# Mixture of experts in a two-block transformer: experts ordered by their tokens, every other one in 64 slots and whole fp32

## Chip, cores and metric

The kernel runs on one core of one Trainium2 chip. The time is that of the device, in microseconds, the median of three runs. One further execution was profiled, and everything about engines and transfers is read from that one.

## The reference

Two transformer blocks follow each other on 256 tokens of width 1024 (and 256 context tokens in the first). The change touches only one step, the mixture of experts in the second layer of the first block:

```python
def swiglu(t, w1, w3, w2):
    return (jax.nn.silu(t @ w1) * (t @ w3)) @ w2

def moe_swiglu(h, w_router, b_router, w1, w3, w2):
    t = h.reshape(-1, shp[-1])
    logits = (t @ w_router).astype(jnp.float32) + b_router.astype(jnp.float32)
    top_v, top_i = lax.top_k(logits, TOP_K)
    top_w = jax.nn.softmax(top_v, axis=-1)
    combine = jnp.sum(jax.nn.one_hot(top_i, N_EXPERTS, dtype=jnp.float32) * top_w[..., None], axis=1)
    y = None
    for e in range(N_EXPERTS):
        ye = combine[:, e:e + 1] * swiglu(t, w1[e], w3[e], w2[e]).astype(jnp.float32)
        y = ye if y is None else y + ye
```

There are 8 experts, each token picks 2, and an expert is 1024 x 2816 twice (w1, w3) and 2816 x 1024 (w2), all in fp32: 34.6 MB.

## The kernel before

Everything is one program whose order on each engine is set by a scheduler that goes by the program's text and its own estimates; each engine then runs its list strictly in that order. Weights come in pieces of 128 x 2048 fp32 (1 MB), issued by SyncE into a ring of raw slots: three slots, and in the expert stage four more (R2), seven in all. Slots are taken in turn, so the load of piece k waits until piece k-7 has left its slot. An expert is 33 pieces: 22 of w1/w3 (each four slices of 128 rows by 256 columns of w1 and 256 of w3) and 11 of w2 (each two slices of 128 rows by 1024 columns).

Products are made to fp32 accuracy out of three faster ones. `piece` (L268) splits a raw piece, 1024 columns at a time, into a high part (ScalarE, L282) and a low part (VectorE, L283), in a second ring `hl` of ten slots, which is room for two and a half pieces; `mm3t` (L294) multiplies high by high, high by low, low by high (L295 to L297), each 128 tokens by 512 columns. I call these split products. A matmul on raw fp32 operands without splitting, a whole product, stands elsewhere in the kernel: in `mod_piece` (L348, four column groups of 32) and in a state sum (L804, two halves of 64 columns).

The stage runs so. The router's scores choose two experts for each token; `sel8` marks them, `rank` numbers the tokens of each expert, `cmb` has their weights. `choice` (L1099) makes `cmb` and `cmax`, the largest count. `gather(e)` (L1120), called for e = 0 and, inside the w2 pass of experts 1, 3 and 5, for the next two, builds a 0/1 matrix `O` of 2 x 128 slots and multiplies it with the split tokens `htk` (L1132, 256 columns), and ScalarE copies the result to `hg` (L1135). Then each expert e, 0 to 7 in that order: 11 steps of two w1/w3 pieces (24 split products into one bank, then silu on ScalarE, the product on VectorE, two transposes on TensorE L1197, and their split L300/L301); then 11 steps of one w2 piece (12 split products, bank S). In step 2 of the next expert, `scatter` (L1138) returns the rows to their tokens, 16 products of 256 columns, and adds them to `accY`. All places have 128 slots. In expert 1 a branch on `cmax` (L1213) calls `overflow`, which would run every expert once more for slots over 128; it is not taken on these inputs. After expert 7 the scatter ends in the residual, the squares of the next norm, and the second block.

## Time and profile before

| | |
|---|---|
| median of 3 runs | 2461.57 us (2458.0 to 2462.22) |
| profiled execution | 2460.61 us |
| its span, first to last instruction | 2458.8 us |
| mean granted TensorE clock | 0.978 of full |
| TensorE busy | 2361.2 us (96%) |
| VectorE, ScalarE busy | 1645.0 us (67%), 1368.0 us (56%) |
| read from HBM | 500.58 MB, 204 GB/s over the span |
| loads of expert weights | 264 of 1024 KB |

Between the span and the execution's time lie 1.8 us. TensorE's busy time is that of overlapping records (a product of 512 columns is drawn with 0.40 us, and the next starts 0.23 us later), so its share says that it always has work, not how much; the distance from start to start is the price of one. The span divides into the first block's two layers up to about 930 us, the experts from 931 to 1751 us, and the second block behind that.

### The profile page before, as it was taken

To read this page: it belongs to the slowest core of one execution; us is meant where nothing else is said; L and a number is where in the kernel's file an instruction comes from. 1 tells how busy PE (TensorE), PEld (TensorE's weight loads), DVE (VectorE), ACT (ScalarE), POOL (GpSimd) and SP (SyncE) were. 2 spreads that over 40 slices of the span, in tenths; PEclk is the share of its full clock that TensorE was granted. 3 is DMA by queue.
4 is the path that set the end of the run, shared out by engine and by line. 5 is a ranking of instruction groups with operands and counts; after the bars stand their busy time and mean duration, and the time that the engine had idled before them with its cause. 6 is when DMAs were issued, how large, how long until landed. Compare 5 with 4: busy or idle time off the path is not lost.

```text
span 2458.8 us, 35481 instructions
## 1 busy us (share of the span) xinstructions
PE 2361.2 (96%) x13906; PEld 2005.0 (82%) x13906; DVE 1645.0 (67%) x2627; ACT 1368.0 (56%) x2186; POOL 5.0 (0%) x12
## 2 busy tenths in 40 slices
PE   6999999999999989999999999999899999999997
PEld 4887777888778877877777788777799999898997
DVE  5655553333366558987988898889766776667765
ACT  4445542232354567876767777677645554455543
POOL 0000000000000000000000000000000000000000
PEclk9999899999999989999999999999999999999999
DMA  8232233333333367987998998888543454333552
GB/s 286 93 122 72 101 120 137 114 127 107 133 113 121 130 235 281 369 318 294 337 352 330 339 346 341 337 348 333 197 146 138 155 188 171 124 144 138 189 180 95
DMA packets 72839, 503.98 MB, mean 205 GB/s; under 512 B 8102, under 2 KB 10188, under 8 KB 14940
## 3 DMA queue, kind: packets, MB, share of 16 engines
q1 hardware_dynamic: 72012, 499.82, 54.9%
q8 instruction: 111, 1.82, 0.3%
q0 software_dynamic: 368, 1.43, 0.2%
q10 hardware_dynamic: 288, 0.41, 0.1%
q14 instruction: 60, 0.49, 0.1%
HBM read 500.58 MB, written 1.06 MB: 204 GB/s over the span
## 4 chain that ended last, share of the span: by engine, by line
PE 49%; DVE 3%; ACT 2%; issue 1%; ACTq 0%; DVEq 0%
PE bkA L290 6%; PE bkA L291 6%; PE bkA L292 6%; PE bkA L296 5%; PE bkA L297 4%; PE bkA L295 4%; PE bkS L295 3%; PE bkS L296 3%; PE bkS L297 3%; PE bkS L290 2%; PE bkS L292 2%; PE bkS L291 2%; DVE hl L283 2%; ACT hl L282 1%; PE bkT L1197 1%
## 5 line engine op out<-in xcount | busy, mean ns | idle before, releaser
L283 DVE TENSOR_TENSOR hl<-raw,hl 128x1024 fp32r<-128x1024 f32 (+2 forms) x861 | 1012.6, 1202 | 386.5 <-ACT hl L282 377.3
L282 ACT CAST hl<-raw 128x1024 fp32r<-128x1024 f32 (+2 forms) x861 | 867.8, 1039 | 424.2 <-PE bkS L291 153.1
L290 PE MATMUL bkA<-ph,hl 128*128 128x256 f32 x1080 | 309.9, 288 | 5.2 <-ACT ph L1356 4.5
L291 PE MATMUL bkA<-pl,hl 128*128 128x256 f32 x1080 | 307.6, 285 | 0.0
L292 PE MATMUL bkA<-ph,hl 128*128 128x256 f32 x1080 | 306.5, 284 | 0.0
L296 PE MATMUL bkA<-hl,hg 128*128 128x512 f32 x704 | 284.3, 404 | 7.1 <-DVE hl L283 5.3
L295 PE MATMUL bkA<-hl,hg 128*128 128x512 f32 x704 | 281.5, 400 | 0.9 <-ACT hl L282 0.9
L297 PE MATMUL bkA<-hl,hg 128*128 128x512 f32 x704 | 282.2, 401 | 0.0
L290 PEld LDWEIGHTS bkA<-ph,hl 128*128 128x128 f32 x1080 | 207.7, 193 | 7.8 <-ACT ph L1356 4.9
L291 PEld LDWEIGHTS bkA<-pl,hl 128*128 128x128 f32 x1080 | 208.0, 193 | 0.3
L292 PEld LDWEIGHTS bkA<-ph,hl 128*128 128x128 f32 x1080 | 207.8, 192 | 0.5 <-issue 0.3
L296 PEld LDWEIGHTS bkA<-hl,hg 128*128 128x128 f32 x704 | 132.7, 189 | 50.4 <-DVE hl L283 22.1
L295 PEld LDWEIGHTS bkA<-hl,hg 128*128 128x128 f32 x704 | 132.8, 189 | 30.3 <-ACT hl L282 2.2
L297 PEld LDWEIGHTS bkA<-hl,hg 128*128 128x128 f32 x704 | 132.9, 189 | 27.1
L296 PE MATMUL bkS<-hl,gh 128*128 128x512 f32 x352 | 140.2, 398 | 6.0 <-PEq L1213 5.3
L290 PE MATMUL bkA<-acth,hl 128*128 128x512 f32 (+1 forms) x376 | 138.7, 369 | 4.4 <-ACT acth L459 4.4
L297 PE MATMUL bkS<-hl,gl 128*128 128x512 f32 x352 | 139.2, 395 | 0.0
L292 PE MATMUL bkA<-acth,hl 128*128 128x512 f32 (+1 forms) x376 | 137.6, 366 | 0.0
L291 PE MATMUL bkA<-actl,hl 128*128 128x512 f32 (+1 forms) x376 | 137.0, 365 | 0.0
L290 PE MATMUL bkS<-acth,hl 128*128 128x512 f32 (+1 forms) x312 | 119.6, 384 | 2.8 <-ACT hl L282 2.8
L295 PE MATMUL bkS<-hl,gh 128*128 128x512 f32 x352 | 121.2, 395 | 0.1
L292 PE MATMUL bkS<-acth,hl 128*128 128x512 f32 (+1 forms) x312 | 119.0, 382 | 0.5 <-DVE hl L283 0.5
(496 smaller groups left out, 4154.9 us busy)
## 6 DMA issues: line engine op xcount, KB each, us to landing
raw<-in_exp_w_dram SPq DMA_DIRECT2D x264, 1024.0 KB, 5.7
raw<-in_w_mod_dram SPq DMA_DIRECT2D x48, 1024.0 KB, 4.9
raw<-in_w_up_dram SPq DMA_DIRECT2D x44, 1024.0 KB, 4.8
raw<-in_w_in_dram SPq DMA_DIRECT2D x32, 1024.0 KB, 4.8
raw<-in_ffn_w_dram SPq DMA_DIRECT2D x30, 1024.0 KB, 4.9
raw<-in_w_out_dram SPq DMA_DIRECT2D x16, 1024.0 KB, 4.8
raw<-in_w_down_dram SPq DMA_DIRECT2D x16, 1024.0 KB, 4.8
raw<-in_w_down_dram SPq DMA_DIRECT2D x8, 768.0 KB, 4.3
```

The source lines that it names most:

```text
L282: SC.copy(hi[:, :m], r)
L283: V.tensor_sub(lo[:, :m], r, hi[:, :m].bitcast(F32))
L290: PE.matmul(o, wh, xh, start=start, stop=False)
L291: PE.matmul(o, wh, xl, start=False, stop=False)
L292: PE.matmul(o, wl, xh, start=False, stop=stop)
L295: PE.matmul(o, th, wh, start=start, stop=False)
L296: PE.matmul(o, th, wl, start=False, stop=False)
L297: PE.matmul(o, tl, wh, start=False, stop=stop)
L1197: PE.transpose(pt[:, c * 128:(c + 1) * 128], g[:, c * 128:(c + 1) * 128], ident)
```

## The change

The experts are put in order of their token counts on the chip, after the router. Place 0 stays expert 0; places 1 to 7 go by falling count. `choice` computes each expert's place by comparing counts (some 27 more small VectorE operations), permutes `rank`, `sel8` and `cmb` into `order`, and writes the expert numbers to `idx`. Loop turn e now works on place `PLACES[e]`: even turns on places 0 to 3, odd ones on places 4 to 7. SyncE reads seven numbers from `idx` into registers, and every load for turns 1 to 7 has its address from a register.

Even turns work as before, with 128 slots. Odd turns (`few`) have 64 slots, and nothing is split: the gather adds the high and low parts on VectorE into one fp32 tile `hg1` of 64 slots (L1180), and the raw piece is the moving operand of whole products (L1250, L1302) with 64 columns of weights. Two such products, for the two halves of the columns, go to partitions 0 to 63 and 64 to 127 of one bank. One transpose a step instead of two, one bank for w2 instead of two, no low part of `yh`, and a scatter of 8 whole products with 64 rows each (L1194). The gathers are made in the w2 pass of the even turns, for turns (0), (1, 2), (3, 4), (5, 6), (7), with 128, 192, 192, 192 and 64 columns. The branch moves from turn 1 to turn 2, and compares counts with each place's capacity.

```diff
+PLACES = (0, 4, 1, 5, 2, 6, 3, 7)
...
+        if name.startswith("exp") and layer in expert_at:
+
+            nc.sync.dma_start(raw[:, :n * w], src.rearrange("(e r) -> e r", r=tot)[
+                ds(expert_at[layer], 1), o:o + 128 * n * w].rearrange("e (p k) -> (e p) k", p=128))
+            return raw, n, w
...
+    def whole(name, i, layer):
+        return (ahead.pop((name, i, layer), None) or load(name, i, layer))[0]
...
+            V.scalar_tensor_tensor(key, p[:, 0:8], 8.0, i8, op0=ALU.mult, op1=ALU.subtract)
+            V.memset(key[:, 0:1], 1.0e6)
+            V.tensor_tensor(t8, key[:, None, :].to_broadcast([128, 8, 8]), key[:, :, None].to_broadcast([128, 8, 8]),
+                            op=ALU.is_gt)
+            V.tensor_reduce(place, t8, axis=AX, op=ALU.add)
...
+            for q, x in enumerate((rank, sel8, cmb)):
+                for t in range(2):
+                    V.tensor_mul(t8, pm, x[:, t, None, :].to_broadcast([128, 8, 8]))
+                    V.tensor_reduce(order[:, q, t, :], t8, axis=AX, op=ALU.add)
...
+            V.tensor_copy(idx, key[0:1, :])
...
-        def gather(e):
+        def gather(es):
...
+            lo_, hi_ = (64 if es[0] % 2 else 128), (128 if es[-1] % 2 else 256)
...
-                        PE.matmul(p[:, v * 256:(v + 1) * 256], htk[:, v, t, d * 128:(d + 1) * 128],
-                                  O[:, t].rearrange("p j s -> p (j s)"), start=t == 0, stop=t == 1)
-                for v in range(2):
-                    last[0] = SC.copy(hg[v][:, d].rearrange("p j s -> p (j s)"), p[:, v * 256:(v + 1) * 256])
...
+                        PE.matmul(p[:, v * 256 + lo_:v * 256 + hi_], htk[:, v, t, d * 128:(d + 1) * 128],
+                                  O[:, t].rearrange("p j s -> p (j s)")[:, lo_:hi_], start=t == 0, stop=t == 1)
+                if hg1 is not None:
+                    V.tensor_reduce(hg1[:, d * 64:(d + 1) * 64], p.rearrange("p (v s) -> p s v", v=2)[:, 64:128, :],
+                                    axis=AX, op=ALU.add)
+                for v in range(2 if hg0 is not None else 0):
+                    last[0] = SC.copy(hg0[:, v, d, :], p[:, v * 256 + 128:(v + 1) * 256])
...
+                    if yl is None:
+                        b = slice(64 * (dd // 4), 64 * (dd // 4) + 64)
+                        PE.matmul(o, yh[b, (dd % 4) * 128:(dd % 4 + 1) * 128], OT[b, :].bitcast(F32), start=True, stop=True)
+                        continue
...
+                if few:
+
+                    for k in range(2):
+                        raw = whole("exp_w13", 2 * i + k, e)
+                        for kc in range(4):
+                            w4 = raw[:, kc * 512:(kc + 1) * 512].rearrange("p (m h c) -> p h m c", m=2, h=2)
+                            for h in range(2):
+                                PE.matmul(p[64 * h:64 * h + 64, :256].rearrange("p (m c) -> p m c", m=2),
+                                          hg1[:, (4 * k + kc) * 64:(4 * k + kc + 1) * 64], w4[:, h],
+                                          start=k == 0 and kc == 0, stop=k == 1 and kc == 3)
...
+                if i == 0 and e == 0:
+                    for v in range(1, 8):
+                        expert_at[v] = nc.values_load(idx[0:1, PLACES[v]:PLACES[v] + 1], engines=[mybir.EngineType.SP],
+                                                      min_val=0, max_val=7)
-                if i == IGA and e == 1:
+                if i == IGA and e == 2:
...
-                if i == IGA and j == 1 and e < 7:
-                    nx = gather(e + 1)
+                if i == IGA and not few:
+                    nx = gather((e + 1, e + 2) if e < 6 else (7,))
...
+                if few:
+                    raw = whole("exp_w2", i, e)
+                    for c in range(2):
+                        for q in range(2):
+                            PE.matmul(yb[0][64 * q:64 * q + 64, :], GT[i][:, c * 64:(c + 1) * 64],
+                                      raw[:, c * 1024 + q * 512:c * 1024 + (q + 1) * 512],
+                                      start=i == 0 and c == 0, stop=i == 10 and c == 1)
+                    continue
```

On TensorE, at the end of turn 0 and the first w1/w3 step of turn 1. Before, behind the last w2 products (bkS), `O` and `cmb` give the weights (L1175) and the transposed `O` (L1180), and then `hl` (the split weights) moves against `hg` (the gathered tokens, high and low), 24 products a step:

```order
L296 MATMUL bkS<-hl,gh 128x512
L297 MATMUL bkS<-hl,gl 128x512
L1175 MATMUL bkT<-cmb,O 128x1 x2
L1180 MATMUL bkT<-cb,O 128x128 x2
L295 MATMUL bkA<-hl,hg_7484 128x512
L296 MATMUL bkA<-hl,hg_7484 128x512
L297 MATMUL bkA<-hl,hg_7485 128x512
```

The same place of the kernel after:

```order
L1230 MATMUL bkT<-order,O 128x1 x2
L1235 MATMUL bkT<-cb,O 128x128 x2
L1250 MATMUL bkA<-raw,hg_8336 64x256 x19
L1256 MATMUL bkT<-cb,g 128x128
L1250 MATMUL bkA<-raw,hg_8336 64x256 x16
```

Sixteen whole products of 256 columns, straight from the raw slot, stand where 24 split products of 512 stood, and the step's transpose comes three products into the next step.

On VectorE, from the end of turn 0's w2 pass into turn 1. Before, the splitting (L283) goes on between the other operations (L1233 the low part of the result, L1194 the product with silu, L301 the low part of its transpose):

```order
L283 TENSOR_TENSOR hl<-raw,hl 128x1024 x19
L1233 SCALAR_TENSOR_TENSOR yl<-bkS,ws,yh 128x512 x2
L1177 COPY ws<-bkT 128x1
L283 TENSOR_TENSOR hl<-raw,hl 128x1024 x4
L1194 TENSOR_TENSOR g<-s,bkA 128x256
L283 TENSOR_TENSOR hl<-raw,hl 128x1024 x2
```

The same place of the kernel after, with the gather's sums (L1180) ahead of it:

```order
L1180 TENSOR_REDUCE hg_8336<-bkT 128x64 x8
L291 TENSOR_TENSOR hl<-raw,hl 128x1024 x11
L1325 SCALAR_TENSOR_TENSOR yl<-bkS,ws,yh 128x512 x2
L1232 COPY ws<-bkT 128x1
L1254 TENSOR_TENSOR g<-s,bkA 128x128 x11
L1232 COPY ws<-bkT 128x1
L291 TENSOR_TENSOR hl<-raw,hl 128x1024 x6
```

In turn 1 nothing is split; the first six halves of pieces of turn 2 are split behind the eleventh product of turn 1, while turn 1 is in its w2 pass.

On SyncE, the loads of turn 0 and the first of turn 1. Before, the one register read is that of `cmax`:

```order
L259 DMA raw<-in_exp_w_dram 128x2048 x10
L1212 TENSOR_LOAD cmax
L1212 ISA x2
L259 DMA raw<-in_exp_w_dram 128x2048 x49
L1213 COMPARE_AND_BRANCH
```

The same place of the kernel after (up to the first of seven reads of `idx`):

```order
L267 DMA raw<-in_exp_w_dram 128x2048 x9
L1289 TENSOR_LOAD cmax
L1289 ISA x2
L267 DMA raw<-in_exp_w_dram 128x2048 x2
L1283 TENSOR_LOAD idx
L1283 ISA x2
```

The reads of `cmax` and of three numbers of `idx` now stand behind the ninth and the eleventh load of turn 0 (the other four follow eleven loads later), and from turn 1 on a register operation stands ahead of each load.

## Rows read from the trace of the kernel before

**Rows 1.** The page: busy us (share) xinstructions; DMA busy in 40 slices.

```profile
PE 2361.2 (96%) x13906; PEld 2005.0 (82%) x13906; DVE 1645.0 (67%) x2627; ACT 1368.0 (56%) x2186; POOL 5.0 (0%) x12
...
DMA  8232233333333367987998998888543454333552
```

**Rows 2.** Stretches, one per expert: us, PE, PEld, DVE, ACT, POOL, clock, DMA, GB/s.

```profile
931.05:1031.88 100.83, 100.83 (x459) 82.42 (x459) 88.04 (x99) 82.48 (x109) 0.00 (x0) 0.98 0.89 336
1031.88:1141.37 109.49, 104.06 (x475) 84.30 (x474) 84.77 (x94) 76.81 (x109) 0.00 (x0) 0.97 0.82 311
1141.37:1241.38 100.01, 99.18 (x443) 78.45 (x443) 88.89 (x100) 72.78 (x92) 0.00 (x0) 1.00 0.91 342
1241.38:1345.34 103.96, 102.37 (x473) 82.24 (x472) 87.89 (x95) 77.71 (x108) 0.00 (x0) 1.00 0.90 337
1345.34:1445.81 100.47, 98.92 (x442) 78.25 (x440) 90.91 (x101) 73.42 (x93) 0.00 (x0) 1.00 0.91 342
1445.81:1548.51 102.70, 102.17 (x473) 82.31 (x472) 86.89 (x94) 76.00 (x107) 0.00 (x0) 1.00 0.89 340
1548.51:1649.13 100.62, 99.13 (x442) 78.33 (x440) 88.97 (x96) 72.98 (x92) 0.00 (x0) 1.00 0.89 346
1649.13:1750.80 101.67, 98.92 (x435) 77.20 (x433) 91.63 (x104) 74.98 (x94) 0.00 (x0) 1.00 0.81 301
```

**Rows 3.** TensorE's timeline, expert 3: start us, us, engine, line, tiles, shape.

```profile
1245.20 0.40 PE L295 MATMUL bkA<-hl,hg 128*128 128x512 f32 x1
1245.44 0.39 PE L296 MATMUL bkA<-hl,hg 128*128 128x512 f32 x1
```

**Rows 4.** Groups by line, expert stage: busy us, mean ns, idle, releaser.

```profile
L283 DVE TENSOR_TENSOR hl<-raw,hl 128x1024 fp32r<-128x1024 f32 x525 | 619.9, 1220 | 76.8 <-ACT hl L282 69.7 <-PE bkA L297 1.4 <-PE bkT L1132 0.8
L282 ACT CAST hl<-raw 128x1024 fp32r<-128x1024 f32 x524 | 529.3, 1058 | 35.8 <-PE bkS L296 26.0 <-PE bkA L296 7.7 <-DVE hl L283 1.2
L296 PE MATMUL bkA<-hl,hg 128*128 128x512 f32 x704 | 284.3, 404 | 7.1 <-DVE hl L283 5.3
```

**Rows 5.** Waits of the DMA queue, experts 2 to 7: us, times, longest.

```profile
SPq L259 <- DVE hl L283: 372.2, 132, 7.4
```

**Rows 6.** Branch in expert 1: TensorE's timeline, a stretch behind it.

```profile
1107.68 0.76 PE L296 MATMUL bkS<-hl,gh 128*128 128x512 f32 x1 [5.33 <-PEq L1213]
...
1106.00:1112.00 6.00, 4.32 (x10) 3.47 (x11) 4.34 (x7) 1.05 (x1) 0.00 (x0) 0.50 0.42 158
```

**Rows 7.** Whole-fp32 products: line 348's timeline, stretches of line 804.

```profile
868.24 1.93 PE L348 MATMUL bkA<-raw,cond 128*32 128x256 f32 x30
870.09 0.50 PE L708 MATMUL bkS<-Kt,qst 128*128 128x512 f32 x1
...
825.47:826.42 0.95, 0.95 (x19) 0.95 (x18) 1.00 0.98 414
826.52:827.46 0.94, 0.94 (x11) 0.70 (x7) 1.00 1.02 418
```

**Rows 8.** TensorE's timeline in the gather of expert 3.

```profile
1320.97 1.12 PE L1132 MATMUL bkT<-O,htk 128*128 128x256 f32 x8
```

**Rows 9.** Stretches with the DMA queue busiest, columns as in rows 2.

```profile
950.00:1030.00 80.00, 80.00 (x357) 64.65 (x356) 74.74 (x78) 63.89 (x77) 0.00 (x0) 1.00 0.97 375
1632.00:1650.00 18.00, 18.00 (x80) 14.74 (x79) 13.58 (x13) 10.88 (x12) 0.00 (x0) 1.00 1.01 414
1430.00:1448.00 18.00, 18.00 (x80) 14.72 (x79) 15.28 (x15) 12.37 (x14) 0.00 (x0) 1.00 0.99 409
1230.00:1243.00 13.00, 12.94 (x57) 10.24 (x55) 9.14 (x9) 7.19 (x9) 0.00 (x0) 1.00 1.01 427
```

**Rows 10.** Small operations: VectorE's timeline, SyncE's register read (ns).

```profile
941.61 0.17 DVE L1106 RECIPROCAL w<-w 128x2 f32<-128x2 f32 x1
...
L1212 SPq TENSOR_LOAD <-cmax x1: 473/473/473, 940.5 to 940.5; - x1
```

**Rows 11.** TensorE's timeline at the end of the expert stage.

```profile
1766.46 0.69 PE L295 MATMUL bkS<-hl,ph 128*128 128x384 f32 x1 [2.90 <-ACT ph L300]
```

More of the change, by code (lines that the diff above doesn't have):

```diff
@@ L261, in load @@
         return raw, n, w
-    ahead, split = {}, {}
+    ahead, split, expert_at = {}, {}, {}
     def prefetch(name, i, layer=None):
@@ L1205, in tile_kernel @@
                     early_table(s)
-            yb = [bank("S"), bank("S")]
+            yb = [bank("S") for _ in range(1 if few else 2)]
             for i in range(11):
-                if i == IGA and e == 1:
+                if i == 0 and e == 0:
[3 more added lines that the diff above has]
+                if i == IGA and e == 2:
                     for k in range(i, i + NPRE):
@@ L1220, in tile_kernel @@
                         given(c, accY[:, c, :])
+                if few:
+                    raw = whole("exp_w2", i, e)
+                    for c in range(2):
+                        for q in range(2):
[3 more added lines that the diff above has]
+                    continue
                 wh, wl = piece("exp_w2", i, e)
```

94 lines of the change are left out of this document (65 added, 29 removed).

## The prediction

> **What bounds the kernel now.** I read the busy line and the slices of the page first: TensorE is busy nearly all the time, and the slices in the middle of the span, where the eight experts run, are the ones in which the DMA engines are busiest as well [rows 1]. So I cut the span at the first w1/w3 product of each expert [rows 2]. The eight stretches run from 931.05 to 1750.80, 819.75 us. In each, TensorE is busy for all but 0 to 5 us, VectorE for 85 to 92 us, and the DMA engines for 0.81 to 0.91 of the time. TensorE sets the pace: its products start 0.23 us apart [rows 3], and one expert has 33 pieces x 12 products = 396, or 396 x 0.234 = 92.7 us of the 100. The splitting of the raw weights is the runner-up, 66 x 1.220 = 80.5 us on VectorE and 66 x 1.058 = 69.8 us on ScalarE for an expert, beside TensorE; in the row of the second of its three w1/w3 products TensorE waited for it 7.1 us in all [rows 4]. The DMA queue is not a bound: it waits for VectorE to free a raw slot (372 us in 600) [rows 5], so all seven slots are full and the next seven pieces are always on their way or there.
>
> From [rows 2] I take three prices. Experts 2, 4 and 6 (no gather inside): 100.0, 100.5, 100.6, mean 100.4. Experts 3 and 5 (one gather): 103.96 and 102.70, so a gather costs 2.9. Expert 1 (gather and branch): 109.49, so the branch costs 109.5 - 100.4 - 2.9 = 6.2; the gap itself is in [rows 6], 5.33 us, and the clock is at half in the stretch behind it.
>
> **The odd experts: products.** Removed are 396 split products (92.7 us) and, on the other two engines, the 66 splits. Added are 176 whole-fp32 products of 256 columns and 44 of 512, half of each kind on either column half. A whole product leaves two records in the trace. How long these take is shown by two kinds of work in this trace. In the w_mod products, 30 records of 256 columns on four column groups are over 1.85 us after the first began [rows 7]; four side by side make eight rounds of at most 0.231 us, and one after another they would have to be 0.06 us each, too short for 256 columns that a split product passes in 0.12 us [rows 8]. And line 804 is the very form that is added, 128x64 weights, whole fp32, outputs on partitions 0 to 63 and 64 to 127: while both halves have work 19 records fall in 0.95 us, when one half alone is left 11 in 0.94 us [rows 7] (both counts include those in flight at the start). So two halves run side by side, and a round of 256 columns costs 0.216 to 0.231 us. w1/w3: 352 records / 2 = 176 rounds, 38.0 to 40.7 us. w2: 88 / 2 = 44 rounds of twice the columns, 19.0 to 20.3 us. Together 57 to 61. To this come 11 transposes that wait for a short chain (silu, product, about 0.3 us each that the three products ahead of them don't cover: 3 us), the change between 64 and 128 columns 22 times (in [rows 7] the next kind begins within a round, so 0.1 to 0.2 us: 2 to 4 us), and the scatter of the expert before (16 x 0.12 = 2 us). TensorE needs 64 to 70 us where it needed 100.4.
>
> The Trainium skill, "TensorEngine Tiling (Array Packing)", Key Properties, says that changing the tiling mode drains TensorE; with a whole drain at each of the 22 changes the expert would take some 4 us more, and no row here shows more than the fraction of a round.
>
> **The odd experts: supply.** With the splits gone, a raw slot is freed by TensorE, and the supply becomes the close second. An expert is 33 pieces of 1.049 MB. The trace shows the queue pressed in short stretches only: 414 and 427 GB/s at a DMA share of 1.01 [rows 9], 2.46 to 2.53 us a piece; over 80 us at a share of 0.97 it is 375 GB/s, 2.80 us [rows 9], but there the slots were the limit, and the gap between landings was VectorE's. I take 2.53, since that stretch is the one in which the queue was pressed longest. An odd expert starts with a ring that is full (7 pieces): 26 x 2.53 = 65.8, with the last piece's products (1.7) and one slot that is not yet filled (2.5) 70 us. The even expert ahead refills the ring: 33 x 2.53 = 83.5 us against its 100 and more. So TensorE (64 to 70) and supply (70) meet, and I take 70 for an odd expert.
>
> **The even experts.** Their products, splits and pieces stay. The gather changes: it is made in expert 0, 2, 4 for two (192 columns) and in 6 for one (64), and a first one of 128 columns ahead of expert 0. No row shows a split product narrower than 256 columns. Lower bound: as now, 2.9 us, since 32 products at 0.12 us [rows 8] lie behind the copies out of the bank. Upper bound: the narrow product passes its columns four times, as whole fp32 does (0.85 ns for a column and two passes, from the 0.216 us of 256): 192 x 1.69 ns = 0.32 us, 32 of them 10.4 us. By kind the nearest row is [rows 8], by width none; I take 7, a little over the middle, and 5 for the gather of 64 columns, and keep both ends. The scatter of an odd expert takes 8 whole products (16 records of 0.216, in two row halves) where 16 short ones stood: +1 us.
>
> The sorting adds some 27 small VectorE operations of about 0.17 us [rows 10], 4.6 us, ahead of expert 0's later splits. VectorE has 13 us left there [rows 2], but the first splits are wanted at once, and the first gather no longer mixes with products: I put 0 to 8 us, and take 4. SyncE reads seven registers, 0.5 us each [rows 10], ahead of expert 0's pieces 11 to 32; behind them the next loads are queued, and whoever waits for these is covered by the pieces already landed (six, or 17 us): nothing. One register operation ahead of each later load is nothing against 2.5 us a piece. The branch moves from expert 1 to expert 2 at its price, 6.2.
>
> **The tail.** The last expert is an odd one. From the end of the last stretch (1750.80) to the first product of the next block, which waits for ScalarE, 15.7 us pass [rows 11], a chain of scatter, residual, square. The scatter's products grow by some 0.4 us for each of four steps; one scaling of 512 columns and all of the low halves go. I put +1.5 us (-1 to +3).
>
> **The sum.** Expert 0: 100.8 + 7 + 4 = 111.8. Expert 2: 100.4 + 6.2 + 7 + 1 = 114.6. Expert 4: 108.4. Expert 6: 100.4 + 5 + 1 = 106.4. Odd: 4 x 70 = 280. Together 721 against 819.75, or 98.5 less; with the tail 97. The profiled execution took 2460.6 us (span 2458.8 and 1.8 around it), which is within 1 us of the median of the runs shown: 2460.6 - 97 = 2364.
>
> **The rivals.** (1) *Supply at the long rate.* If 26 pieces in a row come at 375 GB/s, 2.80 us each, the even experts refill the ring only to about six, and an odd one takes (27 x 2.80) + 4.5 = 80: 4 x 10 more, 2404. For it: no stretch of over 18 us at more than 414. Against it: in all the longer ones slots, not engines, were wanting.
> The Trainium skill, "DMA: Bandwidth & Descriptors", its table at the top, gives 358 GB/s as what HBM has for one core, and further down 425 measured with the neighbour idle. By 358 a piece takes 2.93 us, the ring refills by four, an odd expert takes 90 and the kernel about 2434; the stretches at 409 to 427 in [rows 9] speak for the other figure.
> (2) *TensorE slower in the odd experts*, 77 to 80 us by changes of mode and chains that show: 2392 to 2404.
> (3) *The halves run one after the other* (the other side). Then the odd expert is 352 x 0.216 + 88 x 0.432 = 114 and with the rest 121 to 125; the sum 441 + 4 x 123 = 933, 113 more than before: 2575. It turns slower from 94.6 us an odd expert ((819.75 - 441.2) / 4). Only something that line 804 doesn't have (four times the columns, weights in the moving place straight from a landing slot) could make it so.
> (4) *The gather at its ends:* cheap (3, 3, 3, 2) 2349, dear (10.4 three times, and 3 more ahead of expert 0) 2377. Both belong to the forecast's own range.
> (5) *The change doesn't do what it says:* an expert overflows its place, and the branch runs all eight again with fresh loads, at least 264 x 2.53 = 668 us more, over 3000. On the reference's inputs the router's choices count 67, 52, 81, 77, 60, 56, 61, 58 tokens: the places of 128 get 67, 81, 77, 61, those of 64 get 60, 58, 56, 52. Nothing overflows, unless rounding moves five tokens.
>
> **How the numbers follow.** Forecast with (4) 0.66, (1) 0.17, (2) 0.11, (3) 0.05, (5) 0.01. Predicted is 2364. The range holds the gather's ends, some gain where a stall goes with the splits (TensorE's 4 to 7 us over its own products in an even expert), and most of (1) and (2): 2335 to 2412. Less than 0.2% (5 us) is what a measurement of this kernel can't tell from no change: 0.01 for it, 0.06 slower, 0.93 faster.
>
> **What would show it.** Odd experts of 68 to 72 us in the stretches, with a DMA share near 1 and TensorE's records of lines 1250 and 1302 in two interleaved streams; even experts of 106 to 115. If odd stretches are long with the DMA share well under 1, it is TensorE (rivals 2, 3); long with a share of 1 and under 400 GB/s, the supply. Line 1177's spacing says which end of the gather holds. Wrong altogether if the odd experts come near 95.

## The result

The changed kernel takes 2401.27 us, the median of four runs (2400.18 to 2402.51), against 2461.72 us (2458.0 to 2462.22) for the kernel before on the same chip: a ratio of 0.976 (95% interval 0.974 to 0.978), 60 us less. I had forecast 97 us less. The profiled execution took 2402.21 us, its span 2400.3 us.

The page's busy line and DMA slices after (columns as in [rows 1]):

```profile
PE 2266.7 (94%) x14070; PEld 1848.0 (77%) x14070; DVE 1327.1 (55%) x2365; ACT 1099.8 (46%) x1917; POOL 5.0 (0%) x12
...
DMA  8141323233332445979979989989442555333542
```

VectorE lost 318 us of busy time and ScalarE 268 (the splits of four experts), TensorE 95. The expert stage, slices 17 to 28, has the DMA engines at 7 to 9 tenths as before. The same cut into one stretch per expert as in [rows 2] (us, PE, PEld, DVE, ACT, POOL, clock, DMA share, GB/s); stretches 1, 3, 5 and 7, counted from 0, are those with 64 slots:

```profile
933.00:1047.43 114.43, 112.31 (x490) 91.69 (x490) 90.39 (x133) 81.15 (x121) 0.00 (x0) 0.92 0.78 294
1047.43:1122.98 75.55, 66.77 (x475) 34.59 (x474) 4.39 (x16) 10.74 (x32) 0.00 (x0) 1.00 0.96 394
1122.98:1239.45 116.47, 110.48 (x473) 85.88 (x473) 90.48 (x105) 74.72 (x105) 0.00 (x0) 0.96 0.88 341
1239.45:1316.07 76.62, 67.16 (x474) 34.49 (x473) 8.21 (x24) 8.48 (x28) 0.00 (x0) 1.00 0.96 391
1316.07:1426.73 110.66, 108.06 (x472) 85.05 (x472) 90.61 (x101) 75.34 (x105) 0.00 (x0) 0.97 0.92 356
1426.73:1503.49 76.76, 66.99 (x475) 34.58 (x474) 7.68 (x22) 8.49 (x28) 0.00 (x0) 1.00 0.97 391
1503.49:1609.67 106.18, 105.21 (x472) 83.13 (x472) 88.92 (x101) 71.67 (x89) 0.00 (x0) 0.98 0.94 365
1609.67:1685.67 76.00, 66.02 (x468) 33.95 (x467) 10.45 (x26) 8.34 (x26) 0.00 (x0) 1.00 0.97 393
```

The stage takes 752.7 us where it took 819.75 and where I had 721. Against the forecast, the four odd experts are 24.9 us too long in all (304.9 for 280), the even ones 6.5 (447.7 for 441.2), the start lies 2.0 later, and the tail takes 22.3 us where I had 17.2: 38.5 us, which is the difference between the forecast's span (2362.2) and the measured one, to half a microsecond. Most of it is in the odd experts. Their DMA share is 0.96 to 0.97 and TensorE is idle for 9 to 10 us in each.

**An odd expert, seen closely.** Stretches of turn 1, columns as above, from its start into its last third:

```profile
1047.40:1051.00 3.60, 3.60 (x35) 2.41 (x36) 1.06 (x3) 0.51 (x2) 0.00 (x0) 1.00 0.22 34
1051.00:1055.00 4.00, 4.00 (x35) 2.42 (x33) 0.29 (x1) 0.54 (x2) 0.00 (x0) 1.00 0.95 371
1055.00:1059.00 4.00, 3.75 (x35) 2.23 (x33) 0.29 (x1) 0.54 (x2) 0.00 (x0) 1.00 0.85 307
...
1063.00:1075.00 12.00, 11.45 (x98) 6.84 (x96) 0.72 (x3) 2.41 (x7) 0.00 (x0) 1.00 1.02 425
...
1099.00:1111.00 12.00, 12.00 (x58) 3.97 (x57) 0.00 (x0) 0.37 (x1) 0.00 (x0) 1.00 1.01 421
```

For the first 3.6 us the queue stands (the ring is full and no slot has come free), up to 1059 it is not quite busy, and from then on it moves 416 to 425 GB/s at a share of 1.00 to 1.02 to the end. TensorE's timeline at both ends of the same turn (start, us, engine, line, tiles, shape; idle before it and its releaser):

```profile
1066.84 0.33 PE L1256 MATMUL bkT<-cb,g 128*128 128x128 f32 x1 [0.25 <-DVE g L1254]
1067.10 3.67 PE L1250 MATMUL bkA<-raw,hg 128*64 128x256 f32 x32
...
1071.02 0.33 PE L1256 MATMUL bkT<-cb,g 128*128 128x128 f32 x1 [0.25 <-DVE g L1254]
...
1084.02 0.33 PE L1256 MATMUL bkT<-cb,g 128*128 128x128 f32 x1 [0.70 <-DVE g L1254]
...
1088.65 0.33 PE L1256 MATMUL bkT<-cb,g 128*128 128x128 f32 x1 [0.70 <-DVE g L1254]
...
1099.21 12.24 PE L1302 MATMUL bkS<-raw,gw 128*64 128x512 f32 x56
...
1116.76 1.94 PE L1302 MATMUL bkS<-raw,gw 128*64 128x512 f32 x8 [0.54 <-DMA raw<-in_exp_w_dram]
1119.33 1.94 PE L1302 MATMUL bkS<-raw,gw 128*64 128x512 f32 x8 [0.63 <-DMA raw<-in_exp_w_dram]
1122.98 0.49 PE L306 MATMUL bkA<-hl,hg 128*128 128x512 f32 x1 [1.71 <-ACT hl L290]
```

Two things are to be seen. The 32 records of a w1/w3 step take 3.7 us, so they run in 16 rounds: the halves work side by side. And each part has its own wait. In the w1/w3 steps TensorE waits at the transposes for the chain of silu and product, and nowhere for a piece. In the first of them the transpose stands three products into the next step, as shown under "The change"; TensorE waits 0.25 us there and a step takes 4.19 us from transpose to transpose, where 16 rounds are 3.46. From the sixth wait on it stands right behind its own step's products; the wait is 0.70 us and the step takes 4.63. The longer wait occurs 5, 6, 8 and 11 times in turns 1, 3, 5 and 7, and all these waits add up to 4.7, 5.2, 6.1 and 7.7 us. In w2 the first seven pieces pass without a wait (56 records in 12.24 us); at the last four (in turn 5 the last three) TensorE waits for the weights, one piece every 2.5 us.

**The gather, seen closely.** TensorE, VectorE and ScalarE in the w2 pass of turn 4, columns as in the timeline above; between these rows the splits L290 (1.05 us each) and L291 (1.22 us) run:

```profile
1394.72 0.70 PE L1177 MATMUL bkT<-O,htk 128*128 128x192 f32 x5
1395.01 0.29 DVE L1180 TENSOR_REDUCE hg<-bkT 128x64 f32<-128x128 f32 x1 [0.85 <-PE bkT L1177]
...
1395.33 0.43 ACT L1183 CAST hg<-bkT 128x128 fp32r<-128x128 f32 x2 [2.05 <-DVE hg L1180]
1395.65 1.06 ACT L290 CAST hl<-raw 128x1024 fp32r<-128x1024 f32 x1
1395.82 0.69 PE L1177 MATMUL bkT<-O,htk 128*128 128x192 f32 x4 [0.40 <-ACT hg L1183]
...
1397.15 0.69 PE L1177 MATMUL bkT<-O,htk 128*128 128x192 f32 x4 [0.64 <-ACT hg L1183]
...
1398.69 1.17 PE L1177 MATMUL bkT<-O,htk 128*128 128x192 f32 x4 [0.59 <-ACT hg L1183]
```

Four products of 192 columns take about 0.45 us at the full clock, but the next four come only 1.3 to 1.5 us after them: there are two banks, and each must first be summed by VectorE and copied by ScalarE, both of which do a split in between. TensorE's list has hardly anything else there, and behind these waits its clock is lower:

```profile
1394.50:1398.00 3.50, 2.46 (x16) 1.86 (x14) 2.88 (x5) 2.67 (x6) 0.00 (x0) 1.00 1.02 349
1398.00:1404.00 6.00, 5.41 (x21) 4.63 (x21) 3.81 (x8) 3.17 (x13) 0.00 (x0) 0.54 0.82 332
```

**The tail.** The stretch from the last w2 product to the next block, first before (it ends at the row of [rows 11]), then after:

```profile
1750.80:1766.50 15.70, 8.78 (x34) 5.91 (x33) 8.86 (x21) 6.83 (x17) 1.09 (x2) 0.84 0.41 149
```

```profile
1685.70:1708.00 22.30, 16.78 (x35) 8.24 (x33) 9.01 (x19) 7.52 (x17) 1.09 (x2) 0.56 0.38 139
```

The granted clock is 0.56 after and was 0.84 before; after, the clock is at the lower of its two levels (1.2 and 2.4 GHz) for most of this stretch.

### The profile page after: what moved, and what is told of

It reads as the page before. It is cut to its first block, busy times and chain, and to the rows that moved or that the text cites. A ratio compares the mean times of both kernels' runs of the same rounds, so it can differ in the third digit from the quotient of the medians.

```text
span 2400.3 us, 35435 instructions
## 1 busy us (share of the span) xinstructions
PE 2266.7 (94%) x14070; PEld 1848.0 (77%) x14070; DVE 1327.1 (55%) x2365; ACT 1099.8 (46%) x1917; POOL 5.0 (0%) x12
## 5 line engine op out<-in xcount | busy, mean ns | idle before, releaser
L291 DVE TENSOR_TENSOR hl<-raw,hl 128x1024 fp32r<-128x1024 f32 (+1 forms) x597 | 703.5, 1195 | 410.6 <-ACT hl L290 405.9
L290 ACT CAST hl<-raw 128x1024 fp32r<-128x1024 f32 (+1 forms) x597 | 602.2, 1026 | 428.2 <-PE bkS L302 153.3
L301 PE MATMUL bkA<-ph,hl 128*128 128x256 f32 x1080 | 309.7, 287 | 5.2 <-ACT ph L1448 4.5
L301 PEld LDWEIGHTS bkA<-ph,hl 128*128 128x128 f32 x1080 | 207.4, 192 | 7.8 <-ACT ph L1448 4.9
L1250 PE MATMUL bkA<-raw,hg 128*64 128x256 f32 x1408 | 164.9, 383 | 0.0
L306 PE MATMUL bkA<-hl,hg 128*128 128x512 f32 x352 | 143.5, 408 | 5.3 <-ACT hl L290 5.1
L307 PE MATMUL bkA<-hl,hg 128*128 128x512 f32 x352 | 143.0, 406 | 3.0 <-DVE hl L291 2.3
L308 PE MATMUL bkA<-hl,hg 128*128 128x512 f32 x352 | 143.6, 408 | 0.0
L301 PE MATMUL bkA<-acth,hl 128*128 128x512 f32 (+1 forms) x376 | 138.4, 368 | 4.4 <-ACT acth L470 4.4
L1250 PEld LDWEIGHTS bkA<-raw,hg 128*64 128x64 f32 x1408 | 97.6, 137 | 50.8 <-issue 0.9
L301 PE MATMUL bkS<-acth,hl 128*128 128x512 f32 (+1 forms) x312 | 119.4, 384 | 2.8 <-ACT hl L290 2.8
L302 PE MATMUL bkS<-actl,hl 128*128 128x512 f32 (+1 forms) x312 | 118.2, 379 | 0.0
L1254 DVE TENSOR_TENSOR g<-s,bkA 128x128 f32<-128x128 f32 x44 | 12.7, 289 | 173.1 <-ACT s L1253 173.1
L1302 PE MATMUL bkS<-raw,gw 128*64 128x512 f32 x352 | 79.9, 598 | 8.4 <-DMA raw<-in_exp_w_dram 8.4
L306 PEld LDWEIGHTS bkA<-hl,hg 128*128 128x128 f32 x352 | 67.6, 192 | 24.1 <-ACT hl L290 7.8
```

The lines of the kernel that those rows point to most:

```text
L290: SC.copy(hi[:, :m], r)
L291: V.tensor_sub(lo[:, :m], r, hi[:, :m].bitcast(F32))
L301: PE.matmul(o, wh, xh, start=start, stop=False)
L302: PE.matmul(o, wh, xl, start=False, stop=False)
L306: PE.matmul(o, th, wh, start=start, stop=False)
L307: PE.matmul(o, th, wl, start=False, stop=False)
```

## The experiments

Theory A: the odd experts are set by the arrival of the weights. Theory B: they are set by TensorE's own chain at the transposes. For the even experts, the question was whether the gather costs by its products or by its being one block. This table, worked out from their traces in the way of [rows 2], has the stretches of all of them; "stage" is the sum of the eight, "ratio" is that of the times to the kernel before, with its interval.

| run | median us | ratio | even 0, 2, 4, 6 | odd 1, 3, 5, 7 | stage | tail, clock |
|---|---|---|---|---|---|---|
| the change | 2401.3 | 0.976 (0.974 to 0.978) | 114.4 116.5 110.7 106.2 | 75.5 76.6 76.8 76.0 | 752.7 | 22.3, 0.56 |
| late | 2392.4 | 0.973 (0.971 to 0.976) | 114.3 116.3 112.3 104.9 | 74.6 75.8 74.4 74.6 | 747.2 | 20.9, 0.61 |
| half | 2376.1 | 0.967 (0.964 to 0.969) | 114.2 117.5 113.6 107.6 | 70.3 70.6 70.6 68.0 | 732.4 | 17.0, 0.87 |
| latehalf | 2360.1 | 0.960 (0.957 to 0.963) | 114.3 116.2 113.7 104.9 | 67.5 67.8 67.8 65.2 | 717.3 | 21.7, 0.59 |
| ring8 | 2380.7 | 0.969 (0.967 to 0.970) | 113.4 116.4 112.1 105.8 | 73.2 73.5 74.3 73.8 | 742.5 | 17.3, 0.86 |
| spread | 2381.4 | 0.968 (0.965 to 0.971) | 109.4 116.0 105.0 104.9 | 75.6 76.6 76.8 75.9 | 740.2 | 16.3, 1.00 |
| serial | 2498.1 | 1.014 (1.012 to 1.017) | 115.0 116.5 110.4 107.7 | 99.2 100.4 101.7 101.3 | 852.3 | 22.2, 0.57 |
| static | 2396.3 | 0.973 (0.971 to 0.975) | 115.0 116.8 110.3 106.4 | 75.6 76.4 75.7 75.6 | 751.8 | 20.8, 0.62 |
| all128 | 2473.6 | 1.006 (1.004 to 1.008) | 110.9 109.4 104.9 103.7 | 102.6 102.8 104.2 99.4 | 838.1 | 14.8, 0.93 |
| latespread | 2380.7 | 0.967 (0.965 to 0.970) | 109.4 114.6 105.0 106.4 | 75.0 74.8 74.9 75.0 | 735.1 | 21.1, 0.60 |
| lst | 2375.0 | 0.966 (0.964 to 0.967) | 108.8 115.7 106.4 107.7 | 75.3 75.8 74.8 74.8 | 739.2 | 14.0, 0.95 |
| lstring | 2365.6 | 0.961 (0.959 to 0.963) | 108.8 115.8 105.7 106.0 | 73.1 72.6 73.1 72.5 | 727.6 | 14.0, 1.00 |

A caution for reading it: the stage begins at 925.6 to 933.5 us in these executions, though all the work ahead of it is the same, and the tail's clock differs from run to run. Each of these two differs by up to 8 us between the profiled executions, so I judge an edit by its own stretches first.

### The odd experts: transposes, loads, and both

*late* moves each transpose, in the program's text, behind the next step's products:

```diff
-                    pt = bank("T")
-                    PE.transpose(pt[:, :128], g[:, :128], ident)
-                    gw = mp.tile([128, 256], F32, name="gw", tag="gh", bufs=12)
-                    SC.copy(gw[:, :128], pt[:, :128])
-                    GT.append(gw)
+                    held.append(g)
+                    for g in held[:-1] if i < 10 else held:
+                        pt = bank("T")
+                        PE.transpose(pt[:, :128], g[:, :128], ident)
+                        gw = mp.tile([128, 256], F32, name="gw", tag="gh", bufs=12)
+                        SC.copy(gw[:, :128], pt[:, :128])
+                        GT.append(gw)
+                    held = held[-1:]
```

> In the experts with 64 slots the transposes of a step go behind the products of the next step; nothing else changes. In the trace of the changed kernel a step of w1 and w3 whose weights had come takes 4.19 us from transposes to transposes, of which 16 rounds at 0.216 us are 3.46 and about 0.75 is TensorE waiting for silu, product and the transposes' operand. Theory A (the odd experts are set by the weights' arrival): the transposes' wait only takes the place of a wait for a transfer; at most the first third of each odd expert gets shorter, 1 to 2 us per odd expert, 2393 to 2401 us in all. Theory B (TensorE's own chain of products, silu and transposes sets them): 11 x 0.75 = 8 us less per odd expert, stretches of 68 us instead of 76.5, 2368 us.

*half* leaves out every second load of w1/w3 in the odd experts:

```diff
-                        raw = whole("exp_w13", 2 * i + k, e)
+                        raw = whole("exp_w13", 2 * i, e) if k == 0 else raw
```

> In the experts with 64 slots only every other piece of w1 and w3 is loaded, and is multiplied twice (half of those weights is left out): 22 loads in place of 33, the same work on TensorE. Theory A (arrival of weights): the odd stretches fall to what TensorE asks by itself, 11 x 4.19 + 5 + 44 x 0.43 + 1 = 71 us in place of 76.5, and no wait for a transfer is left in them; about 2380 us. Theory B (TensorE's chain): the odd stretches stay at 75 to 77 us and the time at 2396 to 2402 us.

*latehalf* is both:

> Both edits of the two runs before: the transposes one step later and half of the loads of w1 and w3 in the odd experts left out. Nothing but TensorE's own work is left: 11 x (3.46 + 0.33) + 5 + 19 + 1 = 67 us for an odd expert, 38 us less in all, 2364 us. Theory A (weights): about 4 us per odd expert below the run with half of the loads alone, and far below the run with late transposes alone. Theory B (chain): the same time as the run with late transposes alone, within 4 us.

Turn 3 in late, in half and in latehalf (stretches, columns as before; for the first two a transpose from the middle of the turn's w1/w3 pass):

```profile
1231.90:1307.72 75.82, 67.06 (x474) 34.48 (x473) 8.18 (x24) 8.38 (x28) 0.00 (x0) 1.00 0.97 397
...
1263.38 0.33 PE L1258 MATMUL bkT<-cb,g 128*128 128x128 f32 x1 [0.70 <-DVE g L1254]
```

```profile
1227.57:1298.18 70.61, 66.69 (x474) 34.90 (x473) 8.19 (x24) 8.50 (x28) 0.00 (x0) 1.00 0.72 267
...
1255.69 0.33 PE L1256 MATMUL bkT<-cb,g 128*128 128x128 f32 x1 [0.25 <-DVE g L1254]
```

```profile
1224.71:1292.54 67.83, 66.42 (x475) 35.13 (x474) 8.19 (x24) 8.26 (x28) 0.00 (x0) 1.00 0.76 278
```

By the stretches: late alone gives 5.5 us in four odd experts (304.9 to 299.4), half alone 25.4, both 36.6. Theory B wanted 8 us per odd expert from the late transposes and got 1.4; without the loads' pressure the same edit gives 2.8 (70.3 to 67.5 and so on).

But neither edit did only what I had written, since the scheduler orders TensorE's list anew for each. In late a transpose stands behind the next step's products only in the first steps; in the others it stands right behind its own, with a wait of 0.70 us (the row above), so late did not test theory B in full. Its w1/w3 passes are 5.4 us shorter in the four and its w2 passes as long as before in sum: in turns 1 and 3 the w2 pass is 0.7 and 0.5 longer, as its expectation said, in turns 5 and 7 it is 1.0 and 0.3 shorter. In half the transpose stands three products into the next step throughout (the row above has 0.25 us). So half removed two things: the waits at the transposes fell from 23.7 us in the four experts to 10.1, and those for weights in w2 from 8.4 to nothing. Its 25.4 us are not the weights' alone, and 70 us is what TensorE needs in half's order, not in the change's.

What the weights cost in the change's own order is seen in the next run: 3.1 us in turn 3 and 2.5 in turn 5. Theory A holds in this form: the arrival of the last pieces ends each odd stretch, some 2 to 3 us later than TensorE by itself would, and the change's order on TensorE costs another 3 to 4 us against that of half (73.5 and 74.3 for 70.6 in turns 3 and 5). No run has all the loads and every transpose three products into the next step, so I can't say what that order alone would give. The four medians agree in direction, late's with some help from the start (926.7 for 933.0).

TensorE's timeline in latehalf, where nothing but TensorE is left, shows what a step costs then:

```profile
1250.38 0.33 PE L1258 MATMUL bkT<-cb,g 128*128 128x128 f32 x1
1250.64 3.67 PE L1250 MATMUL bkA<-raw,hg 128*64 128x256 f32 x32
1254.24 0.33 PE L1258 MATMUL bkT<-cb,g 128*128 128x128 f32 x1
```

The step is 3.86 us, 0.40 over the 16 rounds, and 0.26 of that is from the transpose's start to the next product's.

### One more slot in the ring

*ring8* is the other way to test the supply: not fewer loads but one more of them done ahead.

```diff
-NPRE, R2, ISC, IGA = 3+int('42'[0]), (4, 2), 2, 3
+NPRE, R2, ISC, IGA = 8, (5, 1), 2, 3
...
-                    gw = mp.tile([128, 256], F32, name="gw", tag="gh", bufs=12)
+                    gw = mp.tile([128, 256], F32, name="gw", tag="gh", bufs=11)
...
-                    gh_ = mp.tile([128, 256], F32R, name="gh", bufs=12)
-                    gl_ = mp.tile([128, 256], F32R, name="gl", bufs=12)
+                    gh_ = mp.tile([128, 256], F32R, name="gh", bufs=11)
+                    gl_ = mp.tile([128, 256], F32R, name="gl", bufs=11)
```

> One raw slot more (eight) and one slot for split pieces fewer (nine); the room comes from one buffer each of the two rings for transposed products, which have 11 of them where 11 are used. Theory A (the odd experts wait for transfers): each odd expert begins with eight pieces in place of seven, 2.5 us less each, stretches of 73 to 74 us, 2391 us in all, if the even experts bear nine slots. Theory B (the even experts, whose DMA share is 0.92 to 0.94 behind the first, can't fill one piece more, or lose by the ninth slot what the odd ones win): 2398 to 2404 us.

Turn 3 in ring8, and its w2 products on TensorE:

```profile
1229.54:1303.01 73.47, 66.31 (x474) 34.83 (x474) 8.19 (x24) 8.49 (x28) 0.00 (x0) 1.00 0.96 392
...
1282.12 19.18 PE L1302 MATMUL bkS<-raw,gw 128*64 128x512 f32 x88
```

The four odd stretches are 10.1 us shorter (2.3, 3.1, 2.5 and 2.2), in the mean one piece at the queue's rate; the even ones are unchanged in sum (447.7 both times), so nine slots for split pieces were enough. The w1/w3 passes of the odd experts are what they were (211.5 us in the four for 211.9, with 23.3 us of waits at the transposes for 23.7), so the gain is that of the weights. In turns 3 and 5 no w2 product waits for a piece any more: there TensorE's own order sets the stretch, at 73.5 and 74.3 us. The median fell by more (2380.7), with an earlier start (926.5) and a tail of 17.3 us. Theory A as written, for the stretches.

### Are the two halves worth it

*serial* gives the queue the same products, one half of the array at a time:

```diff
-                    for k in range(2):
-                        raw = whole("exp_w13", 2 * i + k, e)
-                        for kc in range(4):
-                            w4 = raw[:, kc * 512:(kc + 1) * 512].rearrange("p (m h c) -> p h m c", m=2, h=2)
-                            for h in range(2):
+                    two = [whole("exp_w13", 2 * i + k, e) for k in range(2)]
+                    for h in range(2):
+                        for k in range(2):
+                            for kc in range(4):
+                                w4 = two[k][:, kc * 512:(kc + 1) * 512].rearrange("p (m h c) -> p h m c", m=2, h=2)
```

> The same w1 and w3 products of the odd experts in another order: first all sixteen of one half of the array, then all sixteen of the other, so that neighbours in the queue stand on the same half and can't run side by side. If the two halves do run side by side in the changed kernel, a step takes 32 rounds of 0.216 us in place of 16, 3.46 us more, 38 us for 11 steps; the weights' arrival, which now sets the odd experts about 6 us later than TensorE would, hides that much: 32 us per odd expert, stretches of about 108 us, 2530 us in all. If the array takes the products of the two halves one after another anyway, the time stays at 2401.

TensorE's timeline in serial, turn 3:

```profile
1291.53 0.33 PE L1256 MATMUL bkT<-cb,g 128*128 128x128 f32 x1 [0.63 <-DVE g L1254]
1291.78 5.51 PE L1250 MATMUL bkA<-raw,hg 128*64 128x256 f32 x32
1297.92 0.33 PE L1256 MATMUL bkT<-cb,g 128*128 128x128 f32 x1 [0.63 <-DVE g L1254]
```

The order of the queue alone makes the kernel slower than the one before: odd stretches of 99 to 102 us, 97.8 us more in the four. So the halves do run side by side in the change, and its gain rests on their neighbours in the queue standing on different halves. My figure of 108 us was too high: 32 records in a row still pass in 5.51 us, not 6.9, since where the list changes from one half to the other some rounds overlap (by the starts of the single records, four rounds at each of the two changes in a step).

### Ordering and addresses

*all128* keeps the ordering and gives every place 128 slots and split products:

```diff
-                few = e % 2 == 1
-                j = 1 - e % 2
+                few = False
+                j = 1
...
-                if i == IGA and not few:
-                    nx = gather((e + 1, e + 2) if e < 6 else (7,))
+                if i == IGA and e < 7:
+                    nx = gather((e + 1,))
```

> The ordering alone: the experts are ordered on the chip and loaded by computed addresses, but all eight have 128 slots and split products, with one gather per expert as in the kernel before. Theory A (the gain is the halved work of four experts, and the ordering costs its start and the branch): eight stretches of about 102.5 us, as before, and 2 to 6 us more for the choice: 2462 to 2470 us. Theory B (the ordering itself costs, by choice and tables in the first two experts and by computed addresses): 2475 us or more.

The expectation says one thing wrongly: the kernel before has one gather for two experts (in turns 1, 3 and 5, [rows 2]), this variant one for each. It came out at 2473.6 us, between the two theories. By pieces: the eight w1/w3 passes take 539.8 us where they took 549.1 before, so the ordering costs them nothing in sum (the first has 72.9 for 69.8); the w2 passes take 298.3 for 270.7. A w2 pass without a gather takes 31 to 32 us, those here with one of 128 columns 36.4 to 38.0 (43.5 with the branch). The loss is the gathers, of which there are more than before, and the gain of the change is not in the order but in the halved work.

*static* puts constants in place of the registers:

```diff
-        if name.startswith("exp") and layer in expert_at:
+        if name.startswith("exp") and layer in expert_at and False:
...
-        base = o + (layer or 0) * tot
+        base = o + (FIXED[layer] if name.startswith("exp") else layer or 0) * tot
```

> The addresses of the experts' weights are constants (the order that the tokens of this input give), while the choice on the chip, the tables and the register loads stay: what is left out is that the loads follow the choice. Theory A (an address from a register costs SyncE some instructions that lie beside the transfers): 2396 to 2403 us, stretches as before it. Theory B (loads with computed addresses are issued later or move slower): the odd stretches, which wait for transfers, fall by 2 us or more each, 2393 us or below.

The stage is 751.8 us for 752.7, and the odd stretches that wait for transfers 303.3 for 304.9. Addresses from registers cost the path nothing that I can tell. Its median (2396.3) lies at the edge of A; the tail was 1.5 us shorter.

### The gather in eight parts

*spread* makes one chunk of the gather at each of the w2 pieces 4 to 11:

```diff
-            for d in range(KC):
+            def chunk(d):
...
+            if later is None:
+                for d in range(KC):
+                    chunk(d)
+            else:
+                later.append(chunk)
...
-                    nx = gather((e + 1, e + 2) if e < 6 else (7,))
+                    later = []
+                    nx = gather((e + 1, e + 2) if e < 6 else (7,), later)
+                if i >= IGA and not few:
+                    later[0](i - IGA)
```

> The gather for the next two experts is no longer one block of 8 chunks at the fourth piece of w2, but one chunk (4 products, its two copies and its reduction) at each of the pieces 4 to 11. In the changed kernel the blocks cost about 10, 10, 10 and 4 us over the plain 31.0 us of w2, though 32 products at 0.113 us are 3.6 us. Theory A (the block waits for ScalarE's copies out of its two banks): a chunk between pieces hides those copies; 5 us less in three even experts, 1 in the last, 2385 us. Theory B (ScalarE and VectorE have that work to do anyway, on top of the splitting of the weights, and TensorE waits for the splits instead): 2398 to 2403 us.

Turn 4's w2 pass, in the change and in spread:

```profile
1385.65:1426.73 41.08, 39.44 (x173) 31.77 (x171) 28.04 (x32) 25.41 (x40) 0.00 (x0) 0.92 0.80 303
```

```profile
1381.00:1416.07 35.07, 35.07 (x173) 28.78 (x171) 26.74 (x32) 24.14 (x40) 0.00 (x0) 1.00 0.91 353
```

The pass takes 35.4 us from its first product (35.07 from 1381.00) in place of 41.1, at a clock of 1.00, and TensorE is never idle. Turn 0 gains the same (41.4 to 35.9). Turn 2 doesn't (44.7 to 44.2): the branch stands there at the same piece, and in TensorE's list most of the chunks still follow each other behind it. Turn 6, with 64 columns, had nothing to give. In sum 12.4 us of the 16 that I expected. A chunk now costs what its four products cost; a chunk's records in the new place:

```profile
1392.62 0.58 PE L1177 MATMUL bkT<-O,htk 128*128 128x192 f32 x4
1393.04 0.41 PE L306 MATMUL bkS<-hl,gh 128*128 128x512 f32 x1
```

0.42 us for four products of 192 columns, 0.105 us each, 3.4 us for 32.

### Together

*latespread* has the late transposes and the spread gather:

> Transposes one step later in the odd experts, and one chunk of the gather per piece of w2 in the even ones. The two touch different stretches: 5.5 us of the odd ones and 12 us of the even ones, as each gave alone; if they add, 2368 to 2382 us with the tail's clock as it comes. If the odd experts only hand their wait on to the next even one (weights arrive no sooner), the sum is no better than the spread gather alone, 2378 to 2384 us.

The stage is 735.1 us, 17.6 less than the change: 5.2 in the odd and 12.3 in the even experts, so the stretches add. The median (2380.7) shows none of late's share over spread, since this run's tail was at 0.60 of the clock (21.1 us) and spread's at 1.00 (16.3).

*lst* adds to it the scatter of an odd expert in pairs, on two banks:

```diff
+                elif q < 2:
+                    both = bank("T"), bank("T")
+                    for d in range(2):
+                        for h in range(2):
+                            b = slice(64 * h, 64 * h + 64)
+                            PE.matmul(both[h][:, d * 256:(d + 1) * 256], yh[b, (2 * q + d) * 128:(2 * q + d + 1) * 128],
+                                      OT[b, :].bitcast(F32), start=True, stop=True)
+                if yl is None:
+                    p = both[q // 2]
```

> Late transposes and the spread gather, and besides in the scatter of an odd expert the two halves' products in pairs, on two banks, so that they can run side by side. Against the run without the last edit (2380.7): if the tail behind the last odd expert is set by the scatter's products at half the clock (0.57 us a record, 16 of them), about half of them goes, 3 to 4 us, 2377 us; if by the chain of residual, square and sum (or the clock alone), nothing, 2379 to 2383.

*lstring* adds the eighth slot to all of it:

> All of these together: late transposes, spread gather, paired scatter, eight raw slots. If the odd experts are still set by the weights' arrival once their transposes are late (stretches of 75 us where TensorE alone needs 67), the eighth slot gives its full 2.5 us in each, about 2367 us. If it gives nothing, 2377 to 2381 us.

The tails of latespread, lst and lstring:

```profile
1665.80:1686.91 21.11, 15.60 (x35) 7.47 (x33) 8.95 (x19) 7.47 (x17) 1.09 (x2) 0.60 0.42 155
```

```profile
1666.97:1680.96 13.99, 8.68 (x34) 4.37 (x32) 8.91 (x19) 7.45 (x17) 1.09 (x2) 0.95 0.57 221
```

```profile
1660.40:1674.38 13.98, 8.67 (x34) 4.37 (x32) 8.91 (x19) 7.45 (x17) 1.09 (x2) 1.00 0.58 223
```

At a clock near 1 the paired scatter's tail is 14.0 us where spread's, unpaired, was 16.3: 2.3 us that I put down to the pairs. I read them from the tail alone, since the stage of lst was 4.1 us longer than that of latespread while its median fell by 5.7. The rest of the difference to latespread is the clock, and whether the pairs also keep the clock up, I can't tell from two runs. The eighth slot takes 9.3 us off the odd stretches (300.6 to 291.3), as it did alone. With all four edits the kernel takes 2365.6 us (2358.5 to 2368.9), 3.9% less than the kernel before and 1.5% less than the change.

## Why the prediction was right, and where it was not

The direction, the mechanism of the gain and the range held (2335 to 2412 holds 2401.3); the forecast itself was 37 us too low, in three terms of the sum, and 2 us are a later start of the stage. The range held because it took in most of rivals 1 and 2: with the forecast's own open term, the gather, it would have ended at 2377. Nor did the odd experts come to the 68 to 72 us that I had named as the sign.

**Odd experts, products: the rounds right, the chain too short.** I had rounds of 0.216 to 0.231 us, side by side, and 64 to 70 us for TensorE. The rows show 0.216 and pairs, and serial shows what their being side by side is worth. But for the waits at the transposes I had 3 us, with three products of the next step ahead of each; most stand right behind their own products, and they cost 4.7 to 7.7 us. With the step into the next expert, which the 64 to 70 don't hold, TensorE needs 73.5 and 74.3 us in the change's order (ring8, turns 3 and 5). Only in half's order it is at 70.3 to 70.6 in turns 1, 3 and 5, and without the chain 2.8 less (latehalf). For the changes of mode I had 2 to 4 us. In latehalf a step has 0.40 us over its rounds for the transpose and both changes together, 4.4 us for an expert, and 0.26 of the 0.40 is from the transpose's start to the next product's. The Trainium skill, "TensorEngine Tiling (Array Packing)", Key Properties, says that a change of tiling mode drains TensorE; by these rows a drain there, if there is one, takes at most 0.2 us a change, less than a round.

**Odd experts, supply: the step that failed, by 25 us.** The rate was right. I took 2.53 us a piece; the queue moved 416 to 425 GB/s at a share of 1.00 to 1.02, 2.47 to 2.52 us. Rival 1, 375 GB/s over the length of an expert, is not what happened, though its 2404 is nearer to the time than my 2364; the mean of 391 to 394 over a stretch is that rate with the queue's idle start in it. The Trainium skill, "DMA: Bandwidth & Descriptors", has 358 GB/s for one core in its table at the top and 425 further down, measured with the neighbour idle; these rows agree with the second. (The 2434 that I had given for the first was added up wrongly: four odd experts that are 20 us longer make 2444.) What was short is the rest of the term, 26 x 2.53 + 1.7 + 2.5 = 70. In turn 1 the last piece's products start at 1119.33, and the stretch up to there is this:

```profile
1047.43:1119.33 71.90, 64.83 (x466) 34.04 (x466) 4.36 (x15) 9.07 (x29) 0.00 (x0) 1.00 0.96 393
```

71.9 us x 393 GB/s are 28.26 MB or 26.9 pieces, which at 421 GB/s (2.49 us each) take 67.0 us. So 4.9 us are the queue's idle time (I had 2.5 for an unfilled slot), and 0.9 of a piece was moved for the next expert (I had none). From there to the next expert's first product are 3.65 us (I had 1.7): the products, the scaling, and 1.71 us in which TensorE waits for the next expert's first split. +1.2, +2.4 and +1.95 make 5.5. Each is small, and the four odd experts are alike, 5.5 to 6.8 us over the 70. And I had taken the larger of two limits that meet at 70. Both were too low: with the supply at 70 as forecast, TensorE's own order would still have made 73.5 and 74.3 us of turns 3 and 5, and the odd experts average 76.2 as built. The two limits are not independent either, since the queue can only load into slots that TensorE has freed: its slow start up to 1059 is the time in which these come one by one.

**Even experts, the gather: mis-sized by 3 us in turns 0 and 4, for a reason that I had named and not priced.** I bounded it between cheap products (2.9) and dear ones (10.4), took 7, and measured 10.4 in turn 0 (41.4 against 31.0), 10.1 in turn 4 and 4.3 in turn 6. The products are at the cheap end, 0.105 us. That turn 0 meets my dear bound of 10.4 is chance, since that was a price of products. The cost is the copies out of two banks (spread, which puts other work between them, saves 5.5 and 5.6 us of it in turns 0 and 4), which my lower bound had waved through as hidden; the narrow gather has one more operation in that chain (the sum on VectorE, ahead of ScalarE's copies), and behind the block's idle time the clock is at 0.54 for the next products. Turn 2, gather and branch, came to 13.7 for 13.2. The sorting's 4 us were 3.3 in turn 0's w1/w3 pass (73.1 for 69.8).

**Addresses, registers: right.** Nothing, by static. **The overflow** (rival 5) didn't occur. **The halves one after another** (rival 3): serial comes nearest to that case, for w1 and w3, at 2498; I had 2575 with w2 in it and the halves strictly in turn.

**The tail: mis-sized by 5 us.** +1.5 was a sum at full clock. At 1.00 (spread) the tail is 16.3 us, +0.65 over 15.65, well within my bounds; at 0.56 it is 22.3. I had let this stretch's clock stay at before's 0.84.

**One row misread.** Of the 7.1 us in [rows 4] only 5.3 are waits for VectorE; nothing in the sum hangs on it.

**Rival 2** (TensorE at 77 to 80 us in the odd experts) gives nearly the stretches that were measured, and a reader of the times alone would take it. It has a part in the truth: the chains do show, and TensorE needs 73 to 74 us, not 70. But it doesn't need 77, the last pieces of w2 are waited for in each odd expert, and ring8 shortens these stretches without a change in their w1/w3 passes.

## To carry over

When an edit brings two limits to the same size, price what each of them loses at the seams (a queue that stands until the first slot comes free, loads for the next stage that share the rate, the step from the last operand to the next stage's first product) and add these, instead of taking the larger limit. When a scheduler sets the order, compare the lists before a difference is read as the share of what you took out: leaving out loads here also moved the transposes. A block of small products that must leave through two banks costs the copies' rhythm, not the products': put it in eight places between other work. When a stretch is supply-bound, buy slots: one more megabyte in the ring was worth 2.2 to 3.1 us an odd expert, in the mean its transfer time, until TensorE's own order was the limit in two of them.

## What the runs showed of the chip

- Two halves of the array overlap not only when their products alternate. With sixteen records of the one half in a row and then sixteen of the other, 32 took 5.51 us where strict turns would need 6.9.
- Products narrower than 256 columns on split operands cost no more than wide ones and little less: 0.105 us for 192 columns in spread, where the eight of 256 in [rows 8] start 0.12 us apart (the next product behind them starts at 1321.93, 0.96 us after the first).
- The tail's clock differed between executions of nearly the same work, 0.56 to 1.00, without an order that I could see: in the change TensorE had waited for transfers just ahead of it (2.3 us in turn 7's w2 pass) and got 0.56, in spread it had waited as long (2.2) and got 1.00, in latehalf it had not waited and got 0.59. What decides it stays open; it is worth 5 to 6 us here.
